# One 512-column product for both token parts in the expert pass, and the gate tables made a step ahead of their products

## The chip, the cores and the metric

The kernel runs on one core of one Trainium2 chip. The metric is the device time of one execution in microseconds, as the median of three runs of the same program.

## The reference, cut to what matters

Two layers over 256 tokens of width 1024. Layer 0 mixes tokens by retention, layer 1 by latent attention; behind each stands the same feed-forward part, which picks 16 of 16384 one-neuron experts for each of 8 heads and each token. Nearly all of the time goes into that part.

```python
def peer_ffn(x, w_q, sub_keys, u, v):          # for each block of 128 tokens
    q = (xb @ w_q).reshape(128, 8, 2, 128)
    s = jnp.einsum('thcd,hckd->thck', q, sub_keys)
    s1, i1 = lax.top_k(s[:, :, 0], 16)
    s2, i2 = lax.top_k(s[:, :, 1], 16)
    ...                                        # best 16 of the 256 sums s1 + s2
    eidx = jnp.take_along_axis(cand_i, pos, axis=-1)   # i1 * 128 + i2
    gate = jax.nn.softmax(top_s, axis=-1)
    h = jax.nn.gelu(jnp.einsum('thkd,td->thk', u[eidx], xb), approximate=False)
    return jnp.einsum('thk,thkd->td', gate * h, v[eidx])
for i in range(2):
    h = layer_norm(DN_ALPHA * h + mix(h), ...)
    h = layer_norm(DN_ALPHA * h + peer_ffn(h, ...), ...)
```

## The kernel before

Experts are not gathered. The kernel computes the hidden values of all 16384 experts for all 256 tokens, multiplies them by a dense gate that is zero where an expert was not picked, and multiplies the result with all of `v`. In each layer the expert part has three stretches: `up(0)` for the first 8192 experts, `up(1)` for the second 8192, and the down pass over 128 weight tiles of `v`. In the profile they lie at about 281 to 462, 462 to 661 and 663 to 1008 us in layer 0, and 1186 to 1372, 1372 to 1567 and 1568 to 1936 us in layer 1.

**Numbers in two parts.** A weight tile (128 x 1024, fp32) is loaded by a DMA that SyncE issues into `raw` (L99). ScalarE (ACT) rounds it to `hi` (L105), and VectorE (DVE) makes the remainder `lo = raw - hi` (L107). The tokens `x` exist as `xh` and `xl` likewise. Of each of `raw`, `hi` and `lo` there are three buffers, so DVE can write the `lo` of a tile only when TensorE (PE) has done its last product with the `lo` of the tile three before it.

**The up pass.** `up(half)` runs over 32 pairs of weight tiles. For each tile `w_stationary` (L121) adds 24 products of 256 columns into PSUM: `hi` with `xh` and with `xl` in turn (16), then `lo` with `xh` (8). Behind each pair ACT reads PSUM and writes the Gelu of it into `H` (L876). PSUM has one bank for a pair, and two such buffers.

**What is woven in.** In `up(0)` the search for the 16 best (many small DVE instructions) is advanced by 1.75 steps a pair. In `up(1)` the generator `densify(0)`, and in the down pass `densify(1)`, make the gates: for each block of 8 tokens DVE writes four tables (`o1` L838, `q` L839, `qh` L840, `ql` L841), PE multiplies them in 16 products of 64 columns into `ps_d` (L848, L849), and DVE multiplies `H` by the result (L854). The 32 products of two blocks stand in one run on PE. There are 16 runs in each `densify`; in `up(1)` most of them have four weight tiles between them, some two. `behind()` sets the place of a generator's step: behind the instruction kept in `latest[0]`, the last `lo`. Within the limits that such marks and the buffers set, a scheduler orders each engine's queue, and each engine takes its queue strictly in order.

**The down pass** (`accumulate_out`, L141) has the 128 tiles of `v` as the moving side, 12 products of 512 columns a tile, into four banks `ys`.

Of the kernel before, what the change touches and what calls it, by code (L numbers as in the profile page):

```python
# [32 lines left out]
NEG = -3.0e38  # L33
TB = 8


def build(tc, A, out):
# [57 lines left out]
    latest_hi = [None]  # L95

    def stream(src, n=1024, slots=None, after=None):
# [16 lines left out]
    def w_stationary(ps, w, ws, x, xs, x_late=False):  # L114

        (wh, wl), (xh, xl) = w, x
        ab = list(zip(ws, xs))
        hh, hl, lh = ([(u, y, a, b) for a, b in ab] for u, y in ((wh, xh), (wh, xl), (wl, xh)))
        todo = hh + lh + hl if x_late else [p for two in zip(hh, hl) for p in two] + lh
        for n, (u, y, a, b) in enumerate(todo):  # L120
            mm(ps, u[:, a : a + P], y[:, :, b, :], start=n == 0, stop=n == len(todo) - 1)  # L121

    def x_stationary(ps, tt, ws, width, x, xs, part=None):

        xh, xl = x
        todo = [(y, w[e], a, b) for y, e in ((xh, 0), (xh, 1), (xl, 0)) for (w, a), b in zip(ws, xs)]
        for n, (y, w, a, b) in enumerate(todo):
            if part is not None and (n >= 20) != part:
                continue
            mm(ps, y[:, tt, b, :], w[:, a : a + width], start=n == 0, stop=n == len(todo) - 1)  # L130

    def accumulate_out(ys, items, first=False, last=False):

        for tt in range(2):
            cols = slice(tt * P, tt * P + P)
            for hf in range(2):
                cf = slice(hf * 512, hf * 512 + 512)
                n = 3 * len(items)
                for (wh, wl), (xh, xl), k in items:
                    for lhs, w in ((xh, wh), (xl, wh), (xh, wl)):  # L140
                        mm(ys[tt][hf], lhs[:, k, cols], w[:, cf], start=first and n == 3 * len(items), stop=last and n == 1)  # L141
                        n -= 1

    def y_banks():
        return [[psum("y", [P, 512], 4) for _ in range(2)] for _ in range(2)]

    def new_x():
        xh = xp.tile([P, 2, ND, P], F32R, tag="xh", name="xh")
        xl = xp.tile([P, 2, ND, P], F32R, tag="xl", name="xl")
        return xh, xl  # L150

# [7 lines left out]
    def layer_norm(ys, s, started, follow=None):  # L159
# [3 lines left out]
        if not last:  # L163
            xh, xl = new_x()
        hv = [slice(hf * 512, hf * 512 + 512) for hf in range(2)]
        for tt in range(2):
# [17 lines left out]
            if tt:  # L184
                first = follow(0, (xh, xl))
                advance(first, 1)
# [11 lines left out]
            if tt:  # L198
                run(first)
                run(follow(1, (xh, xl)))  # L200
        return None if last else (xh, xl)

# [249 lines left out]
    def mla(started, normalise):  # L452
# [9 lines left out]

        cc_ = wp.tile([P, 2, 2, 5, P], F32R, tag="wC", name="cc")
        cc = (cc_[:, 0], cc_[:, 1])
        kr = mp.tile([P, 2, 2, P], F32, tag="kr", name="kr")
# [5 lines left out]
        def compress(tt, x):  # L471
            xh, xl = x
            cps = [psum(tag, [P, b - a]) for a, b, tag in parts]
# [145 lines left out]
        for h in range(8):  # L619
# [10 lines left out]
            if h == 5:  # L630
                tiles = [p_.tile([P, 2, D], F32R, tag=tag, name="tail") for p_, tag in ((xp, "xh"), (xp, "xl"), (wp, "wC"))]
                tail = [(stream(A["mla_w_out"][5 + i], slots=(t[:, 0], t[:, 1])), (oh, ol), 5 + i) for i, t in enumerate(tiles)]
# [16 lines left out]
    def peer(L, wq, normalise, between, tail):  # L649
# [4 lines left out]
        gh = dp.tile([P, T], F16, tag="gh", name="gh", bufs=1)  # L654
        gl = dp.tile([P, T], F16, tag="gl", name="gl", bufs=1)
        ks = list(range(ND))
        fs = [P * k for k in ks]
# [163 lines left out]
        def densify(half):  # L821
# [7 lines left out]
            def tables(ts):  # L829
# [3 lines left out]

                o1 = dp.tile([P, NP, P, 2], F16, tag="o1", name="o1")
                q = dp.tile([P, NP, 64, 2], F16, tag="q", name="q", bufs=1)
                qh = dp.tile([P, NP, 64, 2], F16, tag="qh", name="qh")
                ql = dp.tile([P, NP, 64, 2], F16, tag="ql", name="ql")
                nc.vector.tensor_tensor(o1, columns(slice(0, P), P), of_token(i1T, P), op=ALU.is_equal)  # L838
                nc.vector.tensor_tensor(q, columns(js, 64), of_token(i2T, 64), op=ALU.is_equal)  # L839
                nc.vector.tensor_mul(qh, q, of_token(gh, 64))  # L840
                nc.vector.tensor_mul(ql, q, of_token(gl, 64))  # L841
                return o1, qh, ql

            def products(o1, qh, ql):
                ps = psum("d", [P, TB, 64])
                for t in range(TB):
                    b2, i = t // 2, t % 2
                    mm(ps[:, t], o1[:, b2, :, i], qh[:, b2, :, i], start=True, stop=False)  # L848
                    mm(ps[:, t], o1[:, b2, :, i], ql[:, b2, :, i], start=False, stop=True)  # L849
                return ps  # L850
# [41 lines left out]
        gen = densify(1)  # L892

        def activations(g):
            if g == 0:
                hi = sp.tile([P, 1024], F32R, tag="hi", name="hi", bufs=3).rearrange("p (j t) -> p j t", j=4)
                lo = sp.tile([P, 1024], F32R, tag="lo", name="lo", bufs=3).rearrange("p (j t) -> p j t", j=4)
            else:
                a = xp.tile([P, 2, 4, T], F32R, tag=("xh", "xl")[g % 2], name="a")
                hi, lo = a[:, 0], a[:, 1]  # L900
            split(hi, lo, H[g // 16][:, g % 16 * 4 : g % 16 * 4 + 4])
# [31 lines left out]
        if not tail:  # L933
            t = xp.tile([P, 2, 1024], F32R, tag="xh", name="t")
            items.append((stream(A["peer_v"][L, 124], slots=(t[:, 0], t[:, 1])), a, 0))
# [85 lines left out]
```

## Time and profile before

| | us |
|---|---|
| median of 3 runs | 1946.87 (1943.83 to 1948.31) |
| the profiled execution | 1946.71 |
| its span in the trace | 1944.9 |
| PE busy | 1917.6 (99%) |
| DVE busy | 1456.2 (75%) |
| ACT busy | 896.8 (46%) |

The span runs from the first to the last instruction of the trace; the execution's own time is 1.8 us above it. A share of 99% says that PE hardly ever stands still; it is an average over all stretches, and says nothing yet on how near the other engines are to PE in any one of them.

### The profile page before, as it was taken

Reading aid. Unit: us, or ns where it says so; the run is one execution under the profiler, and the core shown is the slowest. Engines: PE = TensorE matmul, PEld = TensorE weight load, DVE = VectorE, ACT = ScalarE, POOL = GpSimd, SP = SyncE. Lnnn points to the kernel's source line nnn. Section 1 sums busy time; section 2 is a strip of 40 time slices with the busy share of each in tenths; the row PEclk is TensorE's granted clock in tenths of the full one; section 3 lists DMA queues with packets and bytes.
Section 4 is the critical chain, followed back from the end, with each engine's and each line's share of the span. In section 5 each row is a group of like instructions: output and inputs, shape, how many; then the busy total and the mean of one; then the engine's idle time right before and its main releaser. Section 6 shows DMA issues by size and latency. Waiting matters only on the chain. (4 is left out here: it accounts for less than half of the span.)

```text
span 1944.9 us, 34495 instructions
## 1 busy us (share of the span) xinstructions
PE 1917.6 (99%) x13990; PEld 1748.8 (90%) x13990; DVE 1456.2 (75%) x2721; ACT 896.8 (46%) x1052; POOL 29.3 (2%) x52
## 2 busy tenths in 40 slices
PE   8999999999999999999999999999999999999997
PEld 7888899999999988888888889999999988888886
DVE  8666788886777789955667777887777788985555
ACT  5544454544444444445453634454444444444442
POOL 0000000000000000000002000000000000000000
PEclk9999999999999999999999999999999999999999
DMA  6544545555545454556662444555454555555653
GB/s 231 171 162 157 176 160 183 186 183 178 172 164 164 163 184 164 183 188 227 210 228 85 155 148 170 185 181 184 172 169 168 167 169 177 171 178 194 214 194 130
DMA packets 95744, 342.48 MB, mean 176 GB/s; under 512 B 11488, under 2 KB 11872, under 8 KB 95328
## 3 DMA queue, kind: packets, MB, share of 16 engines
q1 hardware_dynamic: 93856, 333.66, 51.8%
q10 hardware_dynamic: 1728, 6.62, 1.0%
q8 instruction: 109, 1.79, 0.4%
q14 instruction: 51, 0.42, 0.1%
HBM read 339.19 MB, written 1.05 MB: 175 GB/s over the span
## 5 line engine op out<-in xcount | busy, mean ns | idle before, releaser
L105 ACT CAST hi<-raw 128x1024 fp32r<-128x1024 f32 x613 | 642.0, 1049 | 908.3 <-PE ps_h L121 462.7
L107 DVE TENSOR_TENSOR lo<-raw,hi 128x1024 fp32r<-128x1024 f32 x613 | 746.6, 1219 | 391.7 <-ACT hi L105 384.5
L121 PE MATMUL ps_h<-xh,hi 128*128 128x256 f32 x2496 | 618.2, 286 | 6.4 <-ACT hi L105 6.1
L121 PE MATMUL ps_h<-xl,hi 128*128 128x256 f32 x2496 | 613.0, 284 | 0.0
L141 PE MATMUL ps_y<-hi,a 128*128 128x512 f32 x1952 | 604.7, 391 | 0.8 <-ACT hi L105 0.7
L121 PEld LDWEIGHTS ps_h<-xh,hi 128*128 128x128 f32 x2496 | 479.8, 192 | 7.3 <-ACT hi L105 6.1
L121 PEld LDWEIGHTS ps_h<-xl,hi 128*128 128x128 f32 x2496 | 480.1, 193 | 0.4
L141 PEld LDWEIGHTS ps_y<-hi,a 128*128 128x128 f32 x1952 | 364.0, 188 | 75.5 <-ACT hi L105 1.5
L141 PE MATMUL ps_y<-lo,a 128*128 128x512 f32 x976 | 381.0, 390 | 0.7 <-DVE lo L107 0.7
L121 PE MATMUL ps_h<-xh,lo 128*128 128x256 f32 x2496 | 352.2, 284 | 2.3 <-DVE lo L107 2.3
L121 PEld LDWEIGHTS ps_h<-xh,lo 128*128 128x128 f32 x2496 | 323.3, 193 | 3.4 <-DVE lo L107 3.1
L141 PEld LDWEIGHTS ps_y<-lo,a 128*128 128x128 f32 x976 | 183.2, 188 | 41.4 <-DVE lo L107 2.8
L838 DVE TENSOR_TENSOR o<-iorep,i1T 128x1024 f16<-128x1024 f16 x128 | 87.5, 684 | 0.0
L854 DVE TENSOR_TENSOR H<-H,ps_d 128x512 f32<-128x512 f32 x128 | 81.7, 679 | 0.0
L112 DVE TENSOR_TENSOR a<-H,a 128x1024 fp32r<-128x1024 f32 x62 | 75.6, 1219 | 3.3 <-ACT a L111 3.2
L876 ACT ACTIVATE H<-ps_h 128x512 f32<-128x512 f32 x128 | 76.5, 597 | 0.1
L848 PEld LDWEIGHTS <-o 128*128 128x128 f16 x1024 | 63.2, 97 | 9.7 <-issue 8.4
L848 PE MATMUL ps_d<-qh,o 128*128 128x64 f16 x1024 | 70.9, 194 | 0.0
L849 PE MATMUL ps_d<-ql,o 128*128 128x64 f16 x1024 | 70.3, 193 | 0.0
L840 DVE TENSOR_TENSOR qh<-q,gh 128x512 f16<-128x512 f16 x128 | 54.0, 422 | 20.7 <-PE ps_d L849 19.3
L111 ACT CAST a<-H 128x1024 fp32r<-128x1024 f32 x62 | 65.0, 1049 | 3.6 <-PE ps_h L121 3.6
L849 PEld LDWEIGHTS <-o 128*128 128x128 f16 x1024 | 64.2, 98 | 0.0
(286 smaller groups left out, 1368.6 us busy)
## 6 DMA issues: line engine op xcount, KB each, us to landing
raw<-in_peer_u_dram SPq DMA_DIRECT2D x256, 512.0 KB, 3.5
raw<-in_peer_v_dram SPq DMA_DIRECT2D x256, 512.0 KB, 4.0
raw<-in_peer_w_q_dram SPq DMA_DIRECT2D x24, 512.0 KB, 3.9
raw<-in_ret_v_dram SPq DMA_DIRECT2D x16, 512.0 KB, 3.5
raw<-in_ret_g_dram SPq DMA_DIRECT2D x16, 512.0 KB, 4.1
raw<-in_ret_w_out_dram SPq DMA_DIRECT2D x16, 512.0 KB, 3.5
raw<-in_ret_q_dram SPq DMA_DIRECT2D x8, 512.0 KB, 4.5
raw<-in_ret_k_dram SPq DMA_DIRECT2D x8, 512.0 KB, 3.6
```

Of the source, the lines that this page charges most:

```text
L105: latest_hi[0] = nc.scalar.copy(hi, raw[:, :n])
L107: latest[0] = nc.vector.tensor_sub(lo, raw[:, :n], hi.bitcast(F32))
L111: nc.scalar.copy(hi, src)
L112: latest[0] = nc.vector.tensor_sub(lo, src, hi.bitcast(F32))
L121: mm(ps, u[:, a : a + P], y[:, :, b, :], start=n == 0, stop=n == len(todo) - 1)
L141: mm(ys[tt][hf], lhs[:, k, cols], w[:, cf], start=first and n == 3 * len(items), stop=last and n == 1)
L838: nc.vector.tensor_tensor(o1, columns(slice(0, P), P), of_token(i1T, P), op=ALU.is_equal)
L840: nc.vector.tensor_mul(qh, q, of_token(gh, 64))
L848: mm(ps[:, t], o1[:, b2, :, i], qh[:, b2, :, i], start=True, stop=False)
L849: mm(ps[:, t], o1[:, b2, :, i], ql[:, b2, :, i], start=False, stop=True)
L854: nc.vector.tensor_mul(hv, hv, ps.rearrange("p t j -> p j t"))
L876: nc.scalar.activation(H[half][:, 2 * jp : 2 * jp + 2], ps, AF.Gelu)
```

## The change

- `xh` and `xl` now lie side by side in one tile (`Parts`), so that both parts of one column block can be the moving side of one product.
- In the up pass `w_stationary_wide` takes the place of `w_stationary`: `hi` with both token parts in one product of 512 columns (8 a tile), then `lo` with `xh` in 8 products of 256 columns. What `hi` gives with `xl` lands in a second half of the bank, so ACT copies that half out for each pair (`cross`), DVE adds it to the first half into `H`, and ACT takes the Gelu in place.
- In `densify` the products of two blocks are issued one round behind their tables, directly behind the last product of a weight tile (`issue_after(latest_mm)`), and the next tile's first product directly behind the last of them (`behind_gates`). `o1`, `qh` and `ql` have three buffers instead of two, `q` is gone: `qh` first holds what `q` held, and is multiplied in place as the last of the four tables.
- The mark `latest[0]` of the up pass is now the pair's addition.

```diff
+    def w_stationary_wide(ps, w, ws, x, xs):
+
+        wh, wl = w
+        for n, (a, b) in enumerate(zip(ws, xs)):
+            with behind_gates() if n == 0 else nullcontext():
+                mm(ps, wh[:, a : a + P], x.both(b), start=n == 0, stop=False)
+        for n, (a, b) in enumerate(zip(ws, xs)):
+            latest_mm[0] = mm(ps[:, 0], wl[:, a : a + P], x.t[:, b, 0], start=False, stop=n == len(ws) - 1)
...
     def y_banks():
-        return [[psum("y", [P, 512], 4) for _ in range(2)] for _ in range(2)]
+        ys = [psum("y", [P, 2, 512]) for _ in range(2)]
+        return [[y[:, hf] for hf in range(2)] for y in ys]
...
-                o1 = dp.tile([P, NP, P, 2], F16, tag="o1", name="o1")
-                q = dp.tile([P, NP, 64, 2], F16, tag="q", name="q", bufs=1)
-                qh = dp.tile([P, NP, 64, 2], F16, tag="qh", name="qh")
-                ql = dp.tile([P, NP, 64, 2], F16, tag="ql", name="ql")
+                o1 = dp.tile([P, NP, P, 2], F16, tag="o1", name="o1", bufs=3)
+                qh = dp.tile([P, NP, 64, 2], F16, tag="qh", name="qh", bufs=3)
+                ql = dp.tile([P, NP, 64, 2], F16, tag="ql", name="ql", bufs=3)
                 nc.vector.tensor_tensor(o1, columns(slice(0, P), P), of_token(i1T, P), op=ALU.is_equal)
-                nc.vector.tensor_tensor(q, columns(js, 64), of_token(i2T, 64), op=ALU.is_equal)
-                nc.vector.tensor_mul(qh, q, of_token(gh, 64))
-                nc.vector.tensor_mul(ql, q, of_token(gl, 64))
+                nc.vector.tensor_tensor(qh, columns(js, 64), of_token(i2T, 64), op=ALU.is_equal)
+                nc.vector.tensor_mul(ql, qh, of_token(gl, 64))
+                nc.vector.tensor_mul(qh, qh, of_token(gh, 64))
...
-            late = []
-            for b in range(0, T // TB, 2):
-                two = [slice((b + i) * TB, (b + i + 1) * TB) for i in range(2)]
-                first = tables(two[0])
-                for one in late:
-                    gate(*one)
-                yield
-                second = tables(two[1])
-                late = list(zip(two, [products(*tabs) for tabs in (first, second)]))
-                yield
-            for one in late:
-                gate(*one)
-            yield
+            blocks = [slice(b * TB, b * TB + TB) for b in range(T // TB)]
+            made = []
+            for b in range(0, len(blocks) + 2, 2):
+                late = []
+                if made:
+
+                    with tc.issue_after(latest_mm[0].ins):
+                        late = [products(*tabs) for tabs in made]
+                made = []
+                if b < len(blocks):
+                    made.append(tables(blocks[b]))
+                    yield
+                for i, ps in enumerate(late):
+                    gate(blocks[b - 2 + i], ps)
+                if b < len(blocks):
+                    made.append(tables(blocks[b + 1]))
+                    yield
...
-                ps = psum("h", [P, 2, T])
+                hs = H[half][:, 2 * jp : 2 * jp + 2]
+                ps = psum("y", [P, 2, 2, T])
                 for i in range(2):
-                    w_stationary(ps[:, i], stream(A["peer_u"][L, half * 64 + 2 * jp + i]), fs, x, ks)
-                nc.scalar.activation(H[half][:, 2 * jp : 2 * jp + 2], ps, AF.Gelu)
+                    w_stationary_wide(ps[:, i], stream(A["peer_u"][L, half * 64 + 2 * jp + i]), fs, x, ks)
+                cross = up_p.tile([P, 2, T], F32, tag="cross", name="cross")
+                nc.scalar.copy(cross, ps[:, :, 1])
+                latest[0] = nc.vector.tensor_add(hs, ps[:, :, 0], cross)
+                nc.scalar.activation(hs, hs, AF.Gelu)
```

What the change does to the queues shows at three places. In the rows, a name's number is that of the buffer's tile: one `lo` number is one weight tile, one `ps_d` number one block of 8 tokens.

First PE in `up(1)` of layer 0, before: the end of a weight tile (`lo_5516`) and the run of gate products behind it. Its second block reads the table `qh_5546`.

```order
L121 MATMUL ps_h_5482<-xh_2224,hi_5515 128x256
L121 MATMUL ps_h_5482<-xl_2225,hi_5515 128x256
L121 MATMUL ps_h_5482<-xh_2224,lo_5516 128x256 x8
L848 LDWEIGHTS o1_5472
L848 MATMUL ps_d_5552<-qh_5474,o1_5472 128x64
...
L849 MATMUL ps_d_5552<-ql_5475,o1_5472 128x64
L848 LDWEIGHTS o1_5544
L848 MATMUL ps_d_5569<-qh_5546,o1_5544 128x64
```

The same kind of place after the change: the end of tile `lo_6783`, the run behind it, and the tiles that follow. The run's second block reads `qh_6751`.

```order
L147 MATMUL ps_y_6757<-xx_2224,hi_6782 128x512 x8
L149 MATMUL ps_y_6757<-xx_2224,lo_6783 128x256 x8
L877 LDWEIGHTS o1_6692
L877 MATMUL ps_d_6806<-qh_6693,o1_6692 128x64
...
L877 MATMUL ps_d_6823<-qh_6751,o1_6750 128x64
...
L147 MATMUL ps_y_6847<-xx_2224,hi_6850 128x512 x8
L149 MATMUL ps_y_6847<-xx_2224,lo_6851 128x256 x8
L147 MATMUL ps_y_6847<-xx_2224,hi_6872 128x512 x8
L149 MATMUL ps_y_6847<-xx_2224,lo_6873 128x256 x8
L147 MATMUL ps_y_6905<-xx_2224,hi_6908 128x512 x8
```

Two products of 256 columns on the same `hi` have become one of 512; the run still stands between two tiles, and the tile that reads `lo_6909` (it goes with `hi_6908`) is the third behind it.

Second DVE at the same two places. Before, the queue around the tables of that second block:

```order
L854 TENSOR_TENSOR H1_2347<-H1_2347,ps_d_5393 128x64x8
L107 TENSOR_TENSOR lo_5516<-raw_5513,hi_5515 128x1024
L838 TENSOR_TENSOR o1_5544<-iorep_83,i1T_2204 128x1024
L839 TENSOR_TENSOR q_5545<-iorep_83,i2T_2205 128x512
L840 TENSOR_TENSOR qh_5546<-q_5545,gh_2206 128x512
L841 TENSOR_TENSOR ql_5547<-q_5545,gl_2207 128x512
L107 TENSOR_TENSOR lo_5590<-raw_5587,hi_5589 128x1024
```

After the change:

```order
L126 TENSOR_TENSOR lo_6851<-raw_6848,hi_6850 128x1024
L912 TENSOR_TENSOR H2_4818<-ps_y_6699,cross_6744 128x512
L883 TENSOR_TENSOR H1_2346<-H1_2346,ps_d_6658 128x64x8
L883 TENSOR_TENSOR H1_2346<-H1_2346,ps_d_6675 128x64x8
L867 TENSOR_TENSOR o1_6750<-iorep_83,i1T_2201 128x1024
L868 TENSOR_TENSOR qh_6751<-iorep_83,i2T_2202 128x512
L126 TENSOR_TENSOR lo_6873<-raw_6870,hi_6872 128x1024
L869 TENSOR_TENSOR ql_6752<-qh_6751,gl_2204 128x512
L126 TENSOR_TENSOR lo_6909<-raw_6906,hi_6908 128x1024
L870 TENSOR_TENSOR qh_6751<-qh_6751,gh_2203 128x512
L912 TENSOR_TENSOR H2_4818<-ps_y_6757,cross_6802 128x512
```

Before, all four tables stood directly behind `lo_5516`, the `lo` of the tile ahead of their run. Now the last of them (`qh_6751`, L870) stands behind `lo_6909`, and the tile three before the one of `lo_6909` is the one of `lo_6783`, directly ahead of the run.

Third DVE after the change at the last run of `up(1)` of layer 0, which stands on PE behind the tile of `lo_7021`; its blocks are `ps_d_7053` and `ps_d_7070`, and the second reads `qh_7047`. The tiles behind `lo_7021` are `lo_7093`, `lo_7115` and `lo_7142`.

```order
L126 TENSOR_TENSOR lo_7142<-raw_7139,hi_7141 128x1024
L912 TENSOR_TENSOR H2_4818<-ps_y_6995,cross_7040 128x512
L883 TENSOR_TENSOR H1_2346<-H1_2346,ps_d_6954 128x64x8
L883 TENSOR_TENSOR H1_2346<-H1_2346,ps_d_6971 128x64x8
L867 TENSOR_TENSOR o1_7046<-iorep_83,i1T_2201 128x1024
L868 TENSOR_TENSOR qh_7047<-iorep_83,i2T_2202 128x512
L883 TENSOR_TENSOR H1_2346<-H1_2346,ps_d_7053 128x64x8
L869 TENSOR_TENSOR ql_7048<-qh_7047,gl_2204 128x512
L867 TENSOR_TENSOR o1_7232<-iorep_83,i1T_2201 128x1024
L870 TENSOR_TENSOR qh_7047<-qh_7047,gh_2203 128x512
```

Here eight more instructions stand between that `lo` and the table. Among the 16 runs of an `up(1)`, 12 look like the second place (one L870 behind a `lo` three tiles on), two like the third (they come two tiles behind the run before them), and in two the last table stands behind a `lo` that is only two tiles on. It is the same in both layers.

## Rows read from the trace of the kernel before

**Rows 1.** The page's head and busy times: engine, us (share of span) x instructions.

```profile
span 1944.9 us, 34495 instructions
...
PE 1917.6 (99%) x13990; PEld 1748.8 (90%) x13990; DVE 1456.2 (75%) x2721; ACT 896.8 (46%) x1052; POOL 29.3 (2%) x52
...
PEclk9999999999999999999999999999999999999999
```

**Rows 2.** What PE waited for, by line: total us, times, longest.

```profile
PE ps_h L121 <- ACT hi L105: 6.1, 1, 6.1
PE ps_h L121 <- DVE lo L107: 2.3, 2, 1.7
```

**Rows 3.** Stretches of up(0) and up(1), layer 0: us, busy of each engine, clock.

```profile
core 0: us, PE busy (x) PEld busy (x) DVE busy (x) ACT busy (x) POOL busy (x), PEclk, DMA share, GB/s
282.00:440.00 158.00, 158.00 (x1319) 158.00 (x1319) 131.88 (x424) 78.42 (x94) 0.00 (x0) 1.00 0.54 181
...
462.00:662.00 200.00, 200.00 (x2041) 199.31 (x2041) 151.11 (x230) 82.40 (x96) 0.00 (x0) 1.00 0.50 166
```

**Rows 4.** The chain that ended last: start, us, engine and line, instructions.

```profile
1187.81 138.23 PE ps_h L121 x1152
...
1379.51 11.59 PE ps_h L121 x96
...
1740.73 168.55 PE ps_y L141 x743
```

**Rows 5.** Timeline of PE at a gate run in up(1): start, us, instruction.

```profile
598.97 0.28 PE L121 MATMUL ps_h<-xl,hi 128*128 128x256 f32 x1
...
599.10 1.12 PE L121 MATMUL ps_h<-xh,lo 128*128 128x256 f32 x8
...
600.06 0.20 PE L848 MATMUL ps_d<-qh,o 128*128 128x64 f16 x1
...
601.03 0.36 PE L121 MATMUL ps_h<-xh,hi 128*128 128x256 f32 x1
...
601.23 0.28 PE L121 MATMUL ps_h<-xl,hi 128*128 128x256 f32 x1
```

**Rows 6.** Timeline of ACT over the same stretch; in brackets the idle time before.

```profile
599.29 1.05 ACT L105 CAST hi<-raw 128x1024 fp32r<-128x1024 f32 x1 [1.83 <-PE ps_h L121]
600.25 0.60 ACT L876 ACTIVATE H<-ps_h 128x512 f32<-128x512 f32 x1
```

**Rows 7.** Timeline of DVE over the same stretch.

```profile
600.38 1.22 DVE L107 TENSOR_TENSOR lo<-raw,hi 128x1024 fp32r<-128x1024 f32 x1 [1.32 <-ACT hi L105]
601.52 0.68 DVE L838 TENSOR_TENSOR o<-iorep,i1T 128x1024 f16<-128x1024 f16 x1
602.12 0.42 DVE L840 TENSOR_TENSOR qh<-q,gh 128x512 f16<-128x512 f16 x1
602.46 0.41 DVE L841 TENSOR_TENSOR ql<-q,gl 128x512 f16<-128x512 f16 x1
602.79 1.27 DVE L854 TENSOR_TENSOR H<-H,ps_d 128x512 f32<-128x512 f32 x2
604.30 1.23 DVE L107 TENSOR_TENSOR lo<-raw,hi 128x1024 fp32r<-128x1024 f32 x1 [0.24 <-ACT hi L105]
```

**Rows 8.** VectorE's groups between 462 and 662 us: busy us, mean ns | idle before, releaser.

```profile
L107 DVE TENSOR_TENSOR lo<-raw,hi 128x1024 fp32r<-128x1024 f32 x63 | 77.1, 1224 | 47.9 <-ACT hi L105 47.7 <-issue 0.2
```

**Rows 9.** Groups over the whole span that read PSUM.

```profile
L854 DVE TENSOR_TENSOR H<-H,ps_d 128x512 f32<-128x512 f32 x128 | 81.7, 679 | 0.0
...
L776 ACT COPY sc<-ps_d 128x512 f32<-128x512 f32 x16 | 9.0, 590 | 4.5 <-PE ps_d L775 4.5
```

**Rows 10.** DMA issues: count, KB each, median us from issue to landing.

```profile
raw<-in_peer_u_dram SPq DMA_DIRECT2D x256, 512.0 KB, 3.5
```

More of the change, by code (lines that the diff above doesn't have):

```diff
@@ L34, with __init__, __getitem__, both @@
 TB = 8
+class Parts:
+    def __init__(self, t):
+        self.t = t
+        self.parts = [t[:, :, e].rearrange("p k (tt t) -> p tt k t", tt=2) for e in range(2)]
+    def __getitem__(self, e):
+        return self.parts[e]
+    def both(self, k):
+        return self.t[:, k]
 def build(tc, A, out):
@@ L95, in build, with behind_gates @@
     latest_hi = [None]
+    latest_mm, latest_gate = [None], [None]
+    def behind_gates():
+        return tc.issue_after(latest_gate[0].ins) if latest_gate[0] is not None else nullcontext()
     def stream(src, n=1024, slots=None, after=None):
@@ L114, in w_stationary @@
     def w_stationary(ps, w, ws, x, xs, x_late=False):
-        (wh, wl), (xh, xl) = w, x
+        (wh, wl), xh, xl = w, x[0], x[1]
         ab = list(zip(ws, xs))
@@ L140, in accumulate_out @@
                     for lhs, w in ((xh, wh), (xl, wh), (xh, wl)):
-                        mm(ys[tt][hf], lhs[:, k, cols], w[:, cf], start=first and n == 3 * len(items), stop=last and n == 1)
+                        with behind_gates() if n == 3 * len(items) else nullcontext():
+                            latest_mm[0] = mm(ys[tt][hf], lhs[:, k, cols], w[:, cf], start=first and n == 3 * len(items), stop=last and n == 1)
                         n -= 1
     def y_banks():
-        return [[psum("y", [P, 512], 4) for _ in range(2)] for _ in range(2)]
+        ys = [psum("y", [P, 2, 512]) for _ in range(2)]
+        return [[y[:, hf] for hf in range(2)] for y in ys]
     def new_x():
-        xh = xp.tile([P, 2, ND, P], F32R, tag="xh", name="xh")
-        xl = xp.tile([P, 2, ND, P], F32R, tag="xl", name="xl")
-        return xh, xl
+        return Parts(xp.tile([P, ND, 2, T], F32R, tag="xx", name="xx"))
     def norm_start(lp, g, b):
@@ L163, in layer_norm @@
         if not last:
-            xh, xl = new_x()
+            x = new_x()
+            xh, xl = x[0], x[1]
         hv = [slice(hf * 512, hf * 512 + 512) for hf in range(2)]
@@ L184, in layer_norm @@
             if tt:
-                first = follow(0, (xh, xl))
+                first = follow(0, x)
                 advance(first, 1)
@@ L199, in layer_norm @@
                 run(first)
-                run(follow(1, (xh, xl)))
-        return None if last else (xh, xl)
+                run(follow(1, x))
+        return None if last else x
     def sincos(pool, cos, sin, ang, n):
@@ L460, in mla @@
         parts = ((0, 384, "h"), (384, 704, "d"))
-        cc_ = wp.tile([P, 2, 2, 5, P], F32R, tag="wC", name="cc")
-        cc = (cc_[:, 0], cc_[:, 1])
+        cc = Parts(wp.tile([P, 5, 2, T], F32R, tag="wC", name="cc"))
         kr = mp.tile([P, 2, 2, P], F32, tag="kr", name="kr")
@@ L471, in compress @@
         def compress(tt, x):
-            xh, xl = x
+            xh, xl = x[0], x[1]
             cps = [psum(tag, [P, b - a]) for a, b, tag in parts]
@@ L630, in mla @@
             if h == 5:
-                tiles = [p_.tile([P, 2, D], F32R, tag=tag, name="tail") for p_, tag in ((xp, "xh"), (xp, "xl"), (wp, "wC"))]
+                t2 = xp.tile([P, 2, 2, D], F32R, tag="xx", name="tail")
+                tiles = [t2[:, 0], t2[:, 1], wp.tile([P, 2, D], F32R, tag="wC", name="tail")]
                 tail = [(stream(A["mla_w_out"][5 + i], slots=(t[:, 0], t[:, 1])), (oh, ol), 5 + i) for i, t in enumerate(tiles)]
@@ L655, in peer @@
         gl = dp.tile([P, T], F16, tag="gl", name="gl", bufs=1)
+        up_p = pool(es, "up", 1)
         ks = list(range(ND))
@@ L848, in products @@
                     mm(ps[:, t], o1[:, b2, :, i], qh[:, b2, :, i], start=True, stop=False)
-                    mm(ps[:, t], o1[:, b2, :, i], ql[:, b2, :, i], start=False, stop=True)
+                    latest_gate[0] = mm(ps[:, t], o1[:, b2, :, i], ql[:, b2, :, i], start=False, stop=True)
                 return ps
@@ L892, in peer @@
         gen = densify(1)
+        aa = [None]
         def activations(g):
+            if g == 1:
+                aa[0] = xp.tile([P, 2, 2, 4, T], F32R, tag="xx", name="a")
             if g == 0:
@@ L898, in activations @@
             else:
-                a = xp.tile([P, 2, 4, T], F32R, tag=("xh", "xl")[g % 2], name="a")
-                hi, lo = a[:, 0], a[:, 1]
+                hi, lo = aa[0][:, g % 2, 0], aa[0][:, g % 2, 1]
             split(hi, lo, H[g // 16][:, g % 16 * 4 : g % 16 * 4 + 4])
@@ L933, in peer @@
         if not tail:
-            t = xp.tile([P, 2, 1024], F32R, tag="xh", name="t")
+            t = aa[0][:, 0].rearrange("p n j t -> p n (j t)")
             items.append((stream(A["peer_v"][L, 124], slots=(t[:, 0], t[:, 1])), a, 0))
```

2 lines of the change are left out of this document (1 added, 1 removed).

## Prediction

> **What bounds the kernel now.** I read the page's head first. PE is busy for 1917.6 of 1944.9 us, at the full clock in every slice [rows 1]. Then I read what PE waits for: the two largest entries are one wait of 6.1 us and two that make 2.3 us [rows 2]. So nothing else has to get faster; a change can gain only by taking products away, and it loses wherever it makes PE wait. The windows tell how far off the next engine is [rows 3]. In `up(0)` DVE is busy for 131.88 of 158 us (83%), in `up(1)` for 151.11 of 200 us (76%); ACT has half its time free. DVE's rest is not a reserve that it can place as it likes: in `up(1)` it stands for 47.7 us in front of `lo`, waiting for the `hi` of the same tile [rows 8], and the `hi` waits until PE has released its buffer [rows 6]. So DVE has run up against the three buffers. It can't write a `lo` before PE is through with the tile three back, however much time it has. That makes the place of each instruction in DVE's queue matter more than DVE's load: what stands behind such a `lo` is tied to the end of a certain tile on PE.
>
> **What the wide products take away.** From the chain, 1152 products of 256 columns follow one another in 138.23 us, 0.1200 us each, and 743 products of 512 columns in 168.55 us, 0.2269 us each [rows 4]. Two short products on one `hi` cost 0.2400 us, the wide one 0.2269: a gain of 0.0131 us each. There are 8 in a tile, 64 tiles in an `up`, and 4 of these: 2048 x 0.0131 = **-27 us**. The tile goes from 24 x 0.1200 = 2.88 to 2.77 us. Both rows are long unbroken runs, so I give this term only 1 us either way.
>
> The Trainium skill ("TensorE: Matmul & The Clock Gate", section "Back-to-back issue gap") gives the isolated gap between warm products as columns/2.4 + 2.5 ns; by it a removed product saves 2.5 ns, and this term would be an estimated 5 us. The rows show 13 ns beyond columns/2.4 at both widths, and they decide the term; what would follow if the smaller saving were true is the last rival.
>
> **What the gate products wait for.** Their number and their grouping don't change: 32 products in a run, from 600.06 to 601.03 us, 0.97 us, and the first product behind costs 0.20 instead of 0.12 us [rows 5]. Half a run is 0.49 us. What changes is what DVE has to do before the second half. In the second place of the queues shown above, PE reaches the run at the end of tile `lo_6783`; call that time T. The second block reads `qh_6751`, whose last writer (L870) stands in DVE's queue behind `lo_6909`. That `lo` takes the buffer that PE was reading up to T. The trace shows the same step: the last product with `hi` starts at 598.97 and takes 0.28 us, ACT starts the next `hi` at 599.29, PE goes on to the run at 600.06, and DVE starts `lo` at 600.38 [rows 5 to 7]. So `lo` starts at T + 0.32. The next DVE instruction starts 1.14 us later (601.52), and a table of 512 elements takes 0.42 us [rows 7]. The table is there at T + 0.32 + 1.14 + 0.42 = T + 1.88, and with some 0.05 us for the signal PE goes on at T + 1.93, where it would have gone on at T + 0.49. **PE stands 1.44 us.** No slack covers this, since each link starts from PE's own end of tile; DVE's load does not enter. Bounds: if `lo` waits for the last product with `lo` alone, T + 0.2 (ACT starts the Gelu at 600.25, 0.19 behind T [rows 6]) gives 1.3 us; if `lo` counts at its full 1.22 us and the signals take 0.2 us each, 1.8 us. There are 12 such runs in each layer: 24 x 1.44 = **+34.6 us** (31 to 43).
>
> At the third place the same `lo` comes first, and eight more stand behind it. From T + 1.46: the addition, two gates, `o1`, one 512-element table, a gate, another such table, another `o1`, then L870. Gates and `o1` read and write as many elements as the rows 601.52 to 602.79 show: 0.60 us apart, small tables 0.34 us [rows 7]; the addition reads PSUM for 512 elements like the gate, and I take 0.60 us for it as well. That makes 6 x 0.60 + 2 x 0.34 = 4.28, and L870 ends at T + 6.16: PE stands 6.21 - 0.49 = 5.7 us. ACT's copy for the addition ends earlier (T + 0.3 + 0.59 [rows 9]). In the other such run two small tables stand in place of a gate and a table, 0.3 us less. I take 5.5 us: 4 x 5.5 = **+22 us** (20 to 26, the upper end with 0.68 us for each of the gates and additions). The two runs a layer whose `lo` is only two tiles on get it 2.8 us earlier and cost nothing. In the kernel before, the four tables of a second block stood behind the `lo` of the tile ahead of the run itself, whose buffer had come free three tiles, some 8.6 us, earlier.
>
> **What else is added.** For each of 128 pairs ACT gets a copy of 0.59 us and DVE an addition, 0.60 to 0.68 us [rows 7, 9]. ACT has room (82 of 200 us busy). On DVE the narrow stretch is `up(0)`. The window of 158 us holds 158/5.76 = 27.4 pairs; 27.4 additions of 0.64 us add 17.5 us, while PE's time falls by 27.4 x 0.21 = 5.8 us. DVE would be busy for 149.4 of 152.2 us, 98% [rows 3]. Instructions back to back overlap a little (1.22 us long, 1.14 apart), so the true load is lower, and what PE reads from DVE there is made ahead by one to two tiles. I take 0.5 us a layer, **+1 us**; from below nothing, from above half of DVE's idle time being unusable: 17.5 + 5.8 - 13 = 10 us a layer. The ring of `raw` holds: a buffer is free once its `lo` is written, and its next `lo` is wanted three tiles later, 3 x 2.77 = 8.3 us. DMA 3.5 [rows 10], `hi` 1.05 and `lo` 1.14 us [rows 6, 7] take 5.7 of them, and one more addition ahead 0.6.
>
> The down pass has the same 12 products a tile as before. There the last table stands three to four tiles ahead of its products, 8 us or more of cover; without it each of 32 runs would cost what a run of `up(1)` does, 46 us. At the turn to the down pass the second pair of banks is wanted 10 products (2.27 us) after the first, and the last addition is done at about T + 2.1: nothing. The side-by-side layout of `x` changes no count of columns elsewhere.
>
> **Sum.** 1946.7 - 27 + 34.6 + 22 + 1 = **1977 us**, 1.6% slower. The profiled execution (1946.71) and the median (1946.87) are the same for this purpose. A difference of 0.2%, 4 us, is about what measurement can tell.
>
> **The rivals.**
> 1. The forecast: PE waits at 28 of 32 runs. By the bounds of its terms, 1970 to 1999; chance 0.70.
> 2. DVE becomes the bound in `up(0)` too. For it: 98% in that window. Against it: the small instructions of the search for the best can slip, as nothing on PE reads them until the end of the stretch. At 10 us a layer: 1977 + 19 = 1996; chance 0.12.
> 3. The other side: the tables come in time. This takes one thing, that the `lo` ahead of L870 is not tied to the tile directly ahead of the run but to one a tile earlier, 2.77 us before, more than the 1.44 us missing; the 4 long waits would shrink to 5.5 - 2.8 each at most, or vanish with the gates ahead of them. Then 1946.7 - 27 + 1 = 1921, or 1932 with what is left of the long ones. For it: in the kernel before PE never waits at a run. Against it: `lo` starts 0.32 us behind the end of a tile in the row, and 43 of 63 rows of `lo` wait like that for a `hi` (47.7 us among them). The point from which it decides: with the long waits in place, the short ones would have to be under 0.2 us each. Chance 0.10.
> 4. Gain and waits cancel: short waits of 0.1 to 0.35 us, or the short ones at half and the long ones gone; 1946 +- 4; chance 0.04.
> 5. The wide product saves only 5 us, since the fixed 13 ns would belong to the `hi` and not to the product: 1977 + 22 = 1999. Against it: both widths show it. Chance 0.04.
>
> **How the numbers follow.** The prediction is the first case. The lower end leaves out the long waits beyond what a short one costs (28 runs) at the lower bound: 1946.7 - 27 + 28 x 1.3 = 1956; the upper end is the first case at its bounds and the second, 1999. Faster 0.10 (rival 3), within 0.2% 0.04 (rival 4), slower 0.86.
>
> **What the profile after would show.** PE's list of waits gets a line for `ps_d` L877 behind DVE `qh` L870, 24 times some 1.4 us and a few times over 5 us, where rows 2 had none. PE's chain in `up(1)` shows runs of gate products cut in the middle, with `lo`, `qh` and signals between. `up(0)` of both layers gets shorter by 64 x 0.105 = 6.7 us, `up(1)` longer by some 22 us. DVE's idle time in front of `lo` in `up(1)` stays. Wrong would be: no wait at L877 (rival 3), `up(0)` not shorter (rival 2 or 5), waits before L147 in `up(0)`, or waits at `ps_y` in the down pass, which I hold to be unchanged.

## The result: 2000.59 us, 2.8% slower

The changed kernel takes 2000.59 us (median of 4 runs, 1999.17 to 2002.43) against 1946.77 us before: a ratio of 1.028, 95% interval 1.0267 to 1.0292. Direction and the place of the waits are as forecast; the time lies 24 us above the predicted 1977 and 1.6 us above the upper end of the range, 1999. The profiled execution took 1999.98 us, with a span of 1998.2.

Head and busy times of the page after, to be held against [rows 1]:

```profile
span 1998.2 us, 30750 instructions
...
PE 1913.0 (96%) x11942; PEld 1649.0 (83%) x11942; DVE 1528.5 (76%) x2849; ACT 969.0 (48%) x1180; POOL 29.3 (1%) x52
...
PEclk9999999999999899999999999999999999999999
```

PE's products cost less, yet the span is 53 us longer, and one slice of the page has a granted clock under 9 tenths, where before none had. What PE waited for after, against [rows 2]:

```profile
PE ps_d L877 <- DVE qh L870: 42.1, 28, 2.5
PE ps_d L877 <- DVE H L883: 10.8, 4, 2.7
...
PE ps_y L149 <- DVE lo L126: 1.8, 3, 0.8
```

Both new lines are the gate products: 28 waits for the last table of a block, 4 for a gate. The first line is the one that the prediction named. The second it did not name: each of the four long waits comes in two parts, one for a gate and one for a table, so that no single wait is over 5 us. Windows of the kernel after, columns as in [rows 3]:

```profile
282.00:440.00 158.00, 157.20 (x899) 137.96 (x898) 145.57 (x468) 94.46 (x122) 0.00 (x0) 1.00 0.53 177
462.00:662.00 200.00, 178.50 (x1378) 156.64 (x1377) 154.58 (x236) 92.18 (x116) 0.00 (x0) 0.98 0.47 154
...
486.00:492.00 6.00, 4.66 (x53) 4.04 (x52) 5.76 (x11) 2.18 (x3) 0.00 (x0) 1.00 0.56 181
...
521.00:526.90 5.90, 3.21 (x32) 2.60 (x30) 4.29 (x6) 2.18 (x3) 0.00 (x0) 1.00 0.42 127
527.00:533.70 6.70, 4.31 (x24) 3.63 (x25) 3.10 (x8) 0.00 (x0) 0.00 (x0) 0.50 0.09 37
...
534.00:540.00 6.00, 6.00 (x38) 5.33 (x37) 3.33 (x4) 3.02 (x4) 0.00 (x0) 1.00 0.26 87
...
1155.00:1158.30 3.30, 3.30 (x10) 2.82 (x11) 3.27 (x6) 1.14 (x2) 0.00 (x0) 0.50 0.00 0
```

`up(0)` is nearly as full as before, `up(1)` has lost 21 of 200 us of PE time. DVE is not the bound there: 155 of 200 us. The small windows are a short wait (full clock), three stretches around a long wait (full, then a granted clock of 0.50, the level of 1.2 GHz, then full again), and the first products of the norm behind the attention stage (0.50).

**A short wait**, row by row; timeline of all engines in `up(1)`, against [rows 5 to 7]:

```profile
487.05 1.05 ACT L124 CAST hi<-raw 128x1024 fp32r<-128x1024 f32 x1 [1.26 <-issue]
...
487.76 0.20 PE L877 MATMUL ps_d<-qh,o 128*128 128x64 f16 x1
...
488.13 1.23 DVE L126 TENSOR_TENSOR lo<-raw,hi 128x1024 fp32r<-128x1024 f32 x1 [0.17 <-ACT hi L124]
...
489.28 0.42 DVE L870 TENSOR_TENSOR qh<-qh,gh 128x512 f16<-128x512 f16 x1
489.61 0.68 DVE L912 TENSOR_TENSOR H<-ps_y,cross 128x512 f32<-128x512 f32 x1
489.75 0.20 PE L877 MATMUL ps_d<-qh,o 128*128 128x64 f16 x1 [1.34 <-DVE qh L870]
...
490.24 1.63 PE L147 MATMUL ps_y<-xx,hi 128*128 128x512 f32 x6
```

With T = 487.76: `lo` at T + 0.37 (forecast 0.32), the table from T + 1.52, PE on again at T + 1.99 (forecast 1.93). From the last product before the run to the first behind it 23 of the 24 short runs take 2.60 to 2.61 us and one takes 2.83; a run with no wait takes 1.09.

**A long wait**; timeline of PE:

```profile
526.25 0.20 PE L877 MATMUL ps_d<-qh,o 128*128 128x64 f16 x1 [2.69 <-DVE H L883]
...
529.39 0.23 PE L877 MATMUL ps_d<-qh,o 128*128 128x64 f16 x1 [2.49 <-DVE qh L870]
...
530.24 3.70 PE L147 MATMUL ps_y<-xx,hi 128*128 128x512 f32 x8
533.78 1.12 PE L149 MATMUL ps_y<-xx,lo 128*128 128x256 f32 x8
534.73 2.00 PE L147 MATMUL ps_y<-xx,hi 128*128 128x512 f32 x8
```

The tile ends at T = 523.40. The first half waits for a gate until T + 2.85, the second for its table until T + 5.99. Then something comes that the prediction does not have: the products of the second half stand 0.053 us apart instead of 0.031, and the next eight wide products take 3.54 us (530.24 to 533.78) instead of 1.84. That is the half clock.

### The profile page after: what moved, and what is told of

Same layout as the page of the kernel before. It is cut to its first block, busy times and chain, and to the rows that moved or that the text cites. A ratio compares the mean times of both kernels' runs of the same rounds, so it can differ in the third digit from the quotient of the medians.

```text
span 1998.2 us, 30750 instructions
## 1 busy us (share of the span) xinstructions
PE 1913.0 (96%) x11942; PEld 1649.0 (83%) x11942; DVE 1528.5 (76%) x2849; ACT 969.0 (48%) x1180; POOL 29.3 (1%) x52
## 3 DMA queue, kind: packets, MB, share of 16 engines
q8 instruction: 93, 1.52, 0.3%
## 5 line engine op out<-in xcount | busy, mean ns | idle before, releaser
L147 PE MATMUL ps_y<-xx,hi 128*128 128x512 f32 x2048 | 522.2, 397 | 0.7 <-ACT hi L124 0.6
L147 PEld LDWEIGHTS ps_y<-xx,hi 128*128 128x128 f32 x2048 | 372.1, 191 | 68.1 <-ACT hi L124 1.1
L149 PEld LDWEIGHTS ps_y<-xx,lo 128*128 128x128 f32 x2048 | 280.1, 191 | 23.6 <-DVE lo L126 3.6
L149 PE MATMUL ps_y<-xx,lo 128*128 128x256 f32 x2048 | 286.8, 283 | 1.9 <-DVE lo L126 1.8
L140 PE MATMUL ps_h<-xx,hi 128*128 128x256 f32 x896 | 121.0, 287 | 6.7 <-ACT hi L124 6.2
L140 PEld LDWEIGHTS ps_h<-xx,hi 128*128 128x128 f32 x896 | 114.2, 194 | 8.5 <-ACT hi L124 6.5
L913 ACT ACTIVATE H<-H 128x512 f32<-128x512 f32 x128 | 80.5, 629 | 64.4 <-DVE H L912 64.3
L912 DVE TENSOR_TENSOR H<-ps_y,cross 128x512 f32<-128x512 f32 x128 | 87.3, 682 | 5.7 <-ACT cross L911 5.7
L911 ACT COPY cross<-ps_y 128x512 f32<-128x512 f32 x128 | 75.0, 586 | 4.8 <-PE ps_y L149 4.6
L140 PE MATMUL ps_h<-xx,lo 128*128 128x256 f32 x448 | 65.5, 289 | 3.1 <-DVE lo L126 3.1
```

The lines of the kernel that those rows point to most:

```text
L147: mm(ps, wh[:, a : a + P], x.both(b), start=n == 0, stop=False)
L149: latest_mm[0] = mm(ps[:, 0], wl[:, a : a + P], x.t[:, b, 0], start=False, stop=n == len(ws) - 1)
L912: latest[0] = nc.vector.tensor_add(hs, ps[:, :, 0], cross)
L913: nc.scalar.activation(hs, hs, AF.Gelu)
```

## The experiments

Theory A: PE loses its time at the runs because a table's place in DVE's queue ties it to the end of the tile ahead of the run. Theory B, the rival: the addition and the copy make DVE the bound, whatever the order.

**The wide products alone**, with the generator of before put back.

```diff
-            blocks = [slice(b * TB, b * TB + TB) for b in range(T // TB)]
-            made = []
...
+            late = []
+            for b in range(0, T // TB, 2):
+                two = [slice((b + i) * TB, (b + i + 1) * TB) for i in range(2)]
+                first = tables(two[0])
...
```

> The wide products with the gate generator of the kernel before. Theory A (the loss comes from the order: a table stands behind a lo that is tied to the tile ahead of the run): in this kernel each block's products stand in a run of their own, and no last table stands behind a lo three tiles on. So the gain of the wide products shows: 256 tiles x 0.087 us = -22, of which up(0) gives back some 5, and twice as many runs cost 32 x 0.2 = 6: about 1935 us (1925 to 1945). Theory B (the addition and the copy make VectorE the bound, whatever the order): the same work is there, so 1970 us or more.

Measured 1941.28 us, ratio 0.9974 (0.9964 to 0.9985): within A's band, 29 us under B's. PE never waits at a gate product.

**The gate generator alone**, put into the kernel before with its narrow products (the edit is against that kernel).

```diff
-            late = []
-            for b in range(0, T // TB, 2):
...
+                    with tc.issue_after(latest_mm[0].ins):
+                        late = [products(*tabs) for tabs in made]
```

> The kernel before with the new gate generator alone, products of 256 columns as before. Theory A: no second block's table stands behind a lo three tiles on; the two runs a layer that follow a double step have seven instructions behind a lo one or two tiles on and may wait 0 to 2 us each: 1947 to 1955 us. If the new arrangement itself cost the time (products behind the last product of a tile, the next tile behind the gates), it would show here too: 1975 us or more.

Measured 1946.08 us, ratio 1.0000 (0.999 to 1.0009). Its `up(1)` of layer 0, window as above:

```profile
462.00:662.00 200.00, 200.00 (x2039) 199.18 (x2038) 153.70 (x232) 83.38 (x96) 0.00 (x0) 1.00 0.54 165
```

PE is full, and the time lies 1 us under the range expected. So neither half loses time by itself. But this kernel keeps the mark of before, the last `lo`, and the run above keeps the generator of before: what the two halves share, and what the changed kernel alone has, is the new generator placed behind the moved mark. The next run takes the mark by itself.

**The mark undone.** One line: the generator's steps are placed behind the last `lo` again, not behind the pair's addition.

```diff
-                latest[0] = nc.vector.tensor_add(hs, ps[:, :, 0], cross)
+                nc.vector.tensor_add(hs, ps[:, :, 0], cross)
```

> The changed kernel with one thing undone: the mark behind which the generator's steps are placed is again the last lo, not the pair's addition. The addition, the copy and every table stay. Theory A (it is the place of the tables in VectorE's queue): now the second block's last table stands behind the lo of the tile ahead of the run itself, whose buffer came free three tiles earlier, so no run waits, and the clock stays up. Without waits the sum is 1946.3 - 22.3 for the wide products + 5 lost again in up(0) + 3 around the attention stage = 1932 us (1929 to 1938). Theory B (VectorE's load): the load is the same, 1960 us or more.

Measured 1932.11 us, ratio 0.9927 (0.9913 to 0.994): faster than before by 0.7%, and 68 us under the changed kernel. DVE's queue around the table of the front's second place now reads:

```
L868 TENSOR_TENSOR qh_6751<-iorep_83,i2T_2202 128x512
L126 TENSOR_TENSOR lo_6783<-raw_6780,hi_6782 128x1024
L869 TENSOR_TENSOR ql_6752<-qh_6751,gl_2204 128x512
L867 TENSOR_TENSOR o1_6840<-iorep_83,i1T_2201 128x1024
L870 TENSOR_TENSOR qh_6751<-qh_6751,gh_2203 128x512
```

The table stands behind `lo_6783`, three tiles earlier than behind `lo_6909`. From the last product before it to the first behind it each of its 16 runs in `up(1)` takes 1.09 us, as one with no wait. The same additions, copies and tables are there, so B falls for `up(1)`. Window and, from 274 to 660 us, the whole list of PE's waits in this kernel:

```profile
462.00:640.00 178.00, 178.00 (x1411) 157.75 (x1409) 155.72 (x243) 92.88 (x117) 0.00 (x0) 1.00 0.56 175
```

```profile
PE ps_y L149 <- DVE lo L126: 0.5, 1, 0.5
```

**Even steps**: no pair takes two steps.

```diff
-        up(1, densify(0), 1.1)
+        up(1, densify(0), 1.0)
```

> The changed kernel with 1.0 instead of 1.1 generator steps a pair in up(1), so that no pair takes two steps and no run follows the one before by two tiles. Theory A: the four long waits (22 us) and the half clock behind them (9 us) go, the short ones stay (26 of them at 1.52 us, 40 us in all): 2000.6 - 22 - 9 + 3 = 1973 us, and no stretch of up(1) at a granted clock under 1. If the clock falls for the many short waits as well, its slices stay under 1 and the time stays over 1980.

Measured 1995.19 us, ratio 1.0245 (1.0228 to 1.0262): 22 us over the expectation. The long waits inside `up(1)` are gone, but a slower generator ends later, and its last run stands behind the last tile. PE in this kernel, timeline:

```profile
677.43 0.20 PE L877 MATMUL ps_d<-qh,o 128*128 128x64 f16 x1 [2.06 <-DVE H L883]
...
680.84 0.23 PE L877 MATMUL ps_d<-qh,o 128*128 128x64 f16 x1 [2.75 <-DVE qh L870]
...
684.67 1.22 PE L170 MATMUL ps_y<-hi 128*128 128x512 f32 x2 [2.80 <-ACT hi L124]
```

One wait of three parts at the end of each `up(1)`, and with it the half clock (0.63 on average from 676 to 690 us). The expectation had overlooked the end of the generator.

**Even steps, `lo` behind the tables.**

```diff
+                tabled.append(nc.vector.tensor_mul(qh, qh, of_token(gh, 64)))
...
-                    w_stationary_wide(ps[:, i], stream(A["peer_u"][L, half * 64 + 2 * jp + i]), fs, x, ks)
+                    w_stationary_wide(ps[:, i], stream(A["peer_u"][L, half * 64 + 2 * jp + i], after=tabled[-3] if half and len(tabled) > 2 else None), fs, x, ks)
```

> As the run with even steps, and each lo of up(1) is put behind the last table made three pairs earlier, so that the last table stands behind a lo two tiles on instead of three. No work is added or taken away. Theory A: no wait at the gate runs is left: 1973 - 40 = 1933 us (1928 to 1940), faster than before. Theory B: VectorE's load is the same, so the waits only move: 1960 us or more.

Measured 1961.41 us, ratio 1.0075 (1.0058 to 1.0092), 34 us under the run above by order alone (40 expected by A). The time itself is 28 us over A's 1933 and lies where B had it, but not for B's reason: the waits did not move. The last run of `up(1)`, which stands in front of the down pass, takes 9.57 us from the last product before it to the first behind it, as it did above (9.58), with the half clock behind it; the 14 runs ahead of it that had waited take 1.34 to 1.35 us, some 0.25 us over one with no wait.

**Steps placed** so that products never follow in the pair of their second table, first with nothing else changed. (It was run after the next two, whose times its expectation uses.)

```diff
-        def up(half, gen, steps):
+        def up(half, gen, steps, twice=()):
...
-                todo += steps
+                todo += steps + (jp in twice)
...
-        up(1, densify(0), 1.1)
+        up(1, densify(0), 1.0, (8, 17, 26))
```

> The changed kernel with nothing else than the steps placed so that no run follows in the pair of its second table and the generator ends two pairs before the down pass. Theory A: the long waits go and with them the half clock in up(1); 16 short waits a layer of 1.5 us stay, since each is tied to the end of its tile: 1935.6 (the same placement without waits) + 32 x 1.5 = 1983 us (1978 to 1987), with the granted clock at 1 all through up(1). If many short waits lower the clock too, there are half-clock slices in up(1) and the time is 1990 or more.

Measured 1968.55 us, ratio 1.0114 (1.0099 to 1.013). The time is lower than expected since only 12 of 16 runs a layer wait, not 16. The clock part holds; `up(1)` of this kernel:

```profile
462.00:670.00 208.00, 192.46 (x1508) 169.39 (x1506) 171.14 (x265) 99.19 (x125) 0.00 (x0) 1.00 0.50 158
```

PE idles for 15.5 us in 12 waits, most of 1.3 us and none over 1.6, and the granted clock is 1.00 throughout.

**The same placement with `lo` behind the tables.** The edit is that of the run above together with an `after=` like that of the run before it; the table that a `lo` stands behind is now looked up by its pair.

> The run with even steps and lo behind the tables, with three pairs that take two steps again, but placed so that the products never follow in the same pair as their second table, and the generator ends two pairs before the down pass. Theory A: the wait of some 8 us at the end of each up(1) and the half clock behind it go; the remainder of 0.25 us a run stays: 1932 + 30 x 0.25 = 1940 us (1935 to 1945). If the wait at the end only moves into the down pass: 1955 us.

Measured 1950.52 us, ratio 1.0017 (1.0008 to 1.0026), 10 us over: the long wait at the end is gone, but in this queue the three runs behind a double step wait, and for a shorter time the last one. PE's waits from 462 to 660 us:

```profile
PE ps_d L878 <- DVE qh L871: 4.4, 4, 1.3
```

**Tables ahead of the gates** in the second step.

```diff
-                for i, ps in enumerate(late):
-                    gate(blocks[b - 2 + i], ps)
                 if b < len(blocks):
                     made.append(tables(blocks[b + 1]))
+                for i, ps in enumerate(late):
+                    gate(blocks[b - 2 + i], ps)
+                if b < len(blocks):
                     yield
```

> As the run with placed steps, with the second block's tables ahead of the two gates in VectorE's queue instead of behind them. Theory A: the last 0.25 us at each run goes, since the table is ready 1.2 us earlier: 1932 us (1929 to 1937). If VectorE is too full for that, the gates come late for the banks of the next run and the time is that of the run before or more.

Measured 1935.56 us, ratio 0.9941 (0.9928 to 0.9955). No wait is left at any run. Two gates, 1.2 us, in front of the table or behind it make 15 us over the 32 runs.

**Without copy and addition.**

```diff
-                cross = up_p.tile([P, 2, T], F32, tag="cross", name="cross")
-                nc.scalar.copy(cross, ps[:, :, 1])
-                latest[0] = nc.vector.tensor_add(hs, ps[:, :, 0], cross)
-                nc.scalar.activation(hs, hs, AF.Gelu)
+                nc.scalar.activation(hs, ps[:, :, 0], AF.Gelu)
```

> As the run with tables first, but the copy and the addition of the second half of the bank are left out (the Gelu takes the first half alone, so the part hi x xl is missing from the output). This prices them: if the 5 us lost in up(0) and the wide product's 0.230 instead of 0.227 us both come from the traffic that they bring, 1932 - 5 - 5 = 1922 us; if only the loss in up(0) does, 1927 us; if neither, 1932 us.

Measured 1929.37 us, ratio 0.9913 (0.9898 to 0.9929): 6 us under the run above, near the middle case. The wide products don't get shorter. Timeline of PE in this kernel, and then in the changed one:

```profile
402.13 2.00 PE L148 MATMUL ps_y<-xx,hi 128*128 128x512 f32 x8
403.98 1.11 PE L150 MATMUL ps_y<-xx,lo 128*128 128x256 f32 x8
404.93 2.00 PE L148 MATMUL ps_y<-xx,hi 128*128 128x512 f32 x8
```

```profile
402.48 2.00 PE L147 MATMUL ps_y<-xx,hi 128*128 128x512 f32 x8
404.32 1.12 PE L149 MATMUL ps_y<-xx,lo 128*128 128x256 f32 x8
405.27 2.00 PE L147 MATMUL ps_y<-xx,hi 128*128 128x512 f32 x8
```

Both have tiles of 2.79 to 2.80 us, 1.84 to 1.85 us of it for eight wide products. The edit also moves the mark to the last `lo`; against the version with only the mark undone (1932.11 us) it gains 2.7 us, and that is nearer to the price of copy and addition, though the two differ in the order of the tables too.

**One bank a tile**, on the version with the mark undone.

```diff
-        ys = [psum("y", [P, 2, 512]) for _ in range(2)]
-        return [[y[:, hf] for hf in range(2)] for y in ys]
+        return [[psum("y", [P, 512], 4) for _ in range(2)] for _ in range(2)]
...
-                ps = psum("y", [P, 2, 2, T])
+                ps = [psum("y", [P, 2, T], 4) for _ in range(2)]
...
-                nc.scalar.copy(cross, ps[:, :, 1])
-                nc.vector.tensor_add(hs, ps[:, :, 0], cross)
+                for i in range(2):
+                    nc.scalar.copy(cross[:, i], ps[i][:, 1])
+                    nc.vector.tensor_add(hs[:, i], ps[i][:, 0], cross[:, i])
```

> The run with the mark on the last lo, with the bank pairs taken apart: four tiles of one bank each instead of two of two banks, and so a copy and an addition for each weight tile instead of one for a pair (256 columns each). If the joint tile is what made the norms behind the down pass and the attention stage start later (VectorE reads the first bank only when the second is done, 1.3 us), these 2.6 us and part of the half clock behind them come back: 1932 - 4 = 1928 us (1925 to 1931). If the halves of copy and addition cost VectorE more than that: 1932 us or more. No change at the gate runs is expected.

Measured 1939.04 us, ratio 0.9962 (0.9949 to 0.9976): 7 us more than with the mark alone undone, and outside the 1925 to 1931 expected. A norm does start earlier (below), but in `up(0)` PE now waits for `lo`. Window, and PE's waits for `lo` in the up pass (8 of the 14 are in `up(0)` of layer 0, 6 in that of layer 1):

```profile
282.00:440.00 158.00, 153.84 (x873) 132.97 (x872) 143.02 (x469) 91.15 (x145) 0.00 (x0) 1.00 0.55 174
```

```profile
PE ps_y L149 <- DVE lo L126: 7.9, 14, 1.0
```

So `up(0)` does not take the additions cut in two without loss. That DVE's load is the reason is not shown: DVE is busy for 143.02 us of this window, and for 145.51 us of it with the mark undone, where PE is busy for 157.45. What grew is the time for which ACT stands in front of the Gelu (L913) until DVE has done the pair's additions. ACT's waits from 282 to 440 us with the mark undone, and then with one bank a tile:

```profile
ACT H L913 <- DVE H L912: 17.0, 17, 2.1
```

```profile
ACT H L913 <- DVE H L912: 35.4, 20, 3.7
```

What stands behind that Gelu on ACT waits with it, and the next `hi` is among it. That is again a place in a queue; load and place are not separated for `up(0)`.

## Why the prediction was right in kind and too low

From equal points of the two traces, the 53.3 us by which the span grew (the measured terms make 53.0, the forecast ones 30.6):

| term | forecast | measured | worked out from |
|---|---|---|---|
| wide products | -27 | -22.3 | 256 tiles x (2.88 - 2.793) |
| 24 short waits | +34.6 | +36.7 | 23 x (2.61 - 1.09) + 1.74 |
| 4 long waits | +22 | +24.0 | 2 x 6.95 + 2 x 7.22 - 4 x 1.09 |
| first tiles behind them | 0 | +6.8 | 4.49, 5.27, 4.63 and 3.95 us instead of 2.88 |
| `up(0)`, beside the wide products | +1 | +4.6 | 183.8 and 183.2 instead of 186.75, where 5.57 were due from each |
| norms, attention, the rest | 0 | +3.2 | the remaining stretches |

**The waits** were right in place, number and size: 24 + 4 at the forecast runs. The long one with the gate ahead of its table was forecast to go on at T + 6.21 and went on at T + 6.25 (674.32, with T = 668.07). The mark-undone run shows the cause by one line of code: nothing is done less, and the waits are gone.

**The step that failed** is the price of a long wait ("PE stands 6.21 - 0.49 = 5.7 us"), as if PE went on afterwards as before. In the run shown above PE idled for 2.69 and, 0.5 us of work later, for 2.49 us; the granted clock went to half in the second of these waits, and what followed ran at half. Over the four long waits that is 6.8 us in the tiles behind the runs, and some 2 us more inside the runs (0.85 instead of 0.49 us a half: in the second half of the run shown, in both halves of the last run of `up(1)`, and likewise in layer 1), so 9 us in all. The even-steps and the placed runs show the same from both sides: the half clock comes where the long wait is, and not with 12 waits of some 1.3 us a layer. These 9 us are the largest part of the 22 by which the forecast fell short. The rest are sizes: 4.7 the wide products, 3.6 `up(0)`, 3.2 the last row, 2.1 the short waits. The time lies 1.6 us above the range, so no one of the larger parts alone put it there; each of them was needed. The Trainium skill ("TensorE: Matmul & The Clock Gate", section "HAM oscillation — how this bites in real kernels") tells of products that start at the low clock again after each wait for data; the trace agrees for the long waits (0.50 behind 2.69 us), and for the short ones it shows 1.00. The prediction did not reckon with it.

**The wide products** saved 10.9 ns for each product taken away (0.087/8), not 13.1. I had taken the length of a 512-column product from the down pass, 0.2269 us; here it is 0.230. It is not the copy's and the addition's doing, as the run without them shows; what it is stays open. The rule that I weighed (the Trainium skill, "TensorE: Matmul & The Clock Gate", section "Back-to-back issue gap", by which 2.5 ns would be saved) is not borne out by this case either, but the bound of 1 us that I gave the term was too narrow.

**`up(0)`** gave back 4.6 us where I took 1 and held 20 possible: DVE is 92% busy in the window, and PE waits there for `lo` and `hi`, 1.6 us in three waits in layer 0. The size is not sharp: the even-steps and the placed run have the same queues in `up(0)`, and theirs take 185.2 and 184.4, and 184.4 and 183.9 us. With the mark undone it is 182.5 and 182.0 us, 2.5 us less in sum, perhaps because there too the small steps had been put behind the addition; the gain is no larger than that scatter. Without copy and addition, the mark on the last `lo` as well, it is 181.2 us in both layers, all that was due.

**The norms** have no term in the prediction; of the stretch ahead of them it says "The down pass has the same 12 products a tile as before". The banks of the down pass and of the attention output are now tiles of two banks each. Timeline of before and after where the attention stage ends:

```profile
1119.60 0.69 DVE L171 SCALAR_TENSOR_TENSOR ln_r<-hres,ps_y 128x512 f32<-128x512 f32 x1 [1.53 <-PE ps_y L141]
...
1120.93 0.67 DVE L171 SCALAR_TENSOR_TENSOR ln_r<-hres,ps_y 128x512 f32<-128x512 f32 x1
...
1125.40 0.66 PE L192 MATMUL ps_h<-ident,hres 128*128 128x128 f32 x4 [0.73 <-DVE hres L179]
```

```profile
1149.32 1.28 DVE L200 SCALAR_TENSOR_TENSOR ln_r<-hres,ps_y 128x512 f32<-128x512 f32 x2 [3.62 <-PE ps_y L170]
...
1154.27 0.66 PE L221 MATMUL ps_h<-ident,hres 128*128 128x128 f32 x4 [1.97 <-DVE hres L208]
```

Before, DVE read the first bank 1.33 us ahead of the second; after, both are read in one go, and PE waits 1.97 instead of 0.73 us. From the last product ahead of the norm to the norm's first it is 2.37 us instead of 1.13. With the banks taken apart it is 1.13 us again; timeline of that run:

```profile
1123.24 0.66 PE L220 MATMUL ps_h<-ident,hres 128*128 128x128 f32 x4 [0.74 <-DVE hres L207]
```

The 3.2 us of the last row are 4.4 lost between the start of layer 0's down pass and layer 1's `up(0)`, where this norm and the half clock behind it lie, and 1.1 gained from the last down pass on. How much of the 4.4 the joint banks cost in all, and where the gain comes from, is open.

Of the rivals, the one on the other side (the tables come in time) did not happen in this kernel, but it is what the mark-undone version does. That its time, 1932 us, is also a number of that rival is luck: there it stood for what is left of the long waits, and this version has none. Without waits the rival's sum was 1921, and the wide products, `up(0)` and the rest make the difference.

## What to carry to other kernels

- An instruction that is free by its engine's load can still be dear by its place: behind a write into a ring of buffers it is tied to the moment at which the other engine frees that buffer. Count from that moment, not from busy shares. Here the mark that sets the place was one line, worth 68 us.
- When a change moves what a helper variable points at (here "the last instruction to stand behind"), read where everything that uses it lands; and when two changes cost nothing alone, look for what they share.
- A wait of some us on TensorE can cost more than itself, because the clock behind it may be at half (here 9 us on four waits, and nothing on waits of 1.3 us); price short and long waits differently.

## What the runs showed of the hardware

- With waits of 2.69 and 2.49 us, 0.5 us of work between them, the granted clock was at 0.50 for 6.7 us (527 to 533.7), though PE was busy for 4.3 of them; with waits of some 1.3 us between 12 us of work it stayed at 1.00. In between it is not settled: behind the 1.97 us in front of the norm it was at 0.50 in the changed kernel (1155 to 1158.3), and at 1.00 behind the same 1.97 us in the run with the tables first.
- Products of 512 columns stood 0.2269 us apart in the down pass of the kernel before and 0.230 in the up pass, there with or without the copy and the addition that read the same banks.
